# Two half steps per couple in the attention pipeline of a two-block kernel

## The chip, the core and the metric

The kernel runs on one core of a Trainium2 chip, as one launch. The metric is the device time of a run in microseconds (us). Five engines of the core work side by side, each through its own queue in order: TensorE (PE; its weight loads are listed apart, as PEld), VectorE (DVE), ScalarE (ACT), GpSimd (POOL) and SyncE (SP), which here issues nearly all the DMAs. They wait for each other through semaphores alone.

## What is computed

256 tokens of width 1024, in float32, go through two models of two layers each. The first block's layer has top-k sparse attention (8 heads), a short convolution, an RWKV-7 recurrence (8 heads) and a gated feed-forward part. The second block's layer, which most of the change concerns, is this:

```python
u = hdn @ w_in
qa, ka, va, za, qb, kb, vb, zb, ga, gb = split_cols(u)
ya = dilated_mixture(qa, ka, va)                  # 16 heads of 64
ya = ya * jax.nn.silu(za)
ob = diff_attention(qb[0::2], qb[1::2], kb[0::2], kb[1::2], vb, lam)   # 8 heads, two softmaxes each
yb = rms_norm_2(ob, subln_w, SUBLN_EPS) * (1.0 - lam_init) * jax.nn.silu(zb)
merged = jax.nn.sigmoid(ga) * (ya @ w_proj_a) + jax.nn.sigmoid(gb) * (yb @ w_proj_b)
return x + merged @ w_out
```

`yb @ w_proj_b` needs all heads of the second attention, `ya @ w_proj_a` all of the first, and everything else in `u` needs neither.

## The kernel before

Every weight product is done in three passes of a reduced float32: the weights are loaded by DMA into `raw` and split by ACT (L184, `whi`) and DVE (L185, `wlo`) into a high and a low part; PE multiplies the parts by those of the activations, in the token-major form (L244 to L246, 512 columns each) or the feature-major one (L206 to L208, 256 columns). A "weight product" below is one such matmul. There are two buffers of `raw`, three of `whi`, three of `wlo`, and three PSUM banks (`mm`) for the results.

An attention is cut into couples of softmaxes, each in three pieces. The scores piece (`softmax_pair`): PE writes scores (L445), DVE evicts them with the mask and the row's extreme (L451), ACT takes the exponential (L454), DVE the reciprocal of the sum (L457). The probabilities piece: DVE scales (L465; in the second attention also L1411 and L1414), PE transposes (L486), ACT copies the result (L488, `pt`). The products piece: PE multiplies by the values (L496 and L498 in the first block and in the dilated attention, L1421 to L1423 in the differential one), and ACT takes the result out (L1424) and sums its squares (L1427). One half of an attention in the second block, `half`, is four couples. After the four couples of a half of the differential attention come a reciprocal root (`rstd`, L275 with L261 to L271), eight products on DVE (L1437), eight transposes (L393) and the split of the result (L1359, L1360), which the second half of the rows of `w_proj_b` multiplies.

`pipelined` runs four couples so that in step i the scores of couple i, the products of couple i-2 and the probabilities of couple i-1 are issued. It is a generator. Each number it yields is a length in a planner's units: `interleave` keeps a clock for each stream of work, advances the stream that is earliest, and so writes the program's order. In the second block two streams run, `bulk` with the weight products, which yields 10.4 after a token-major group of 48 and 5.2 after a feature-major one, and `attend`, whose step is `2 * TUNE["a2"]` or `2 * TUNE["b2"]` (9.95 and 10.49). In the first block there are three, `rwkv`, `attend` with `2 * TUNE["a1"]` times 0.746, and `bulk`. Streams also stop for each other: in the second block `bulk` does not begin the projection by `w_proj_b` before `attend` has finished, and in the first it does not begin the attention's gate and branch products before that. Within this order a compile-time scheduler may still move an instruction ahead where its inputs are ready earlier.

In the first block's recurrence a solve on DVE ends in transposes (L933, L935), then PE, ACT and DVE hand each other small steps: L942, L947 (the inverse), and for each of four stretches of tokens L962 and L965, L972, L977, L990 and L993.

In the second block, 176.8 of the planner's units of `bulk` stand ahead of the projections in the first layer, and each projection has 20.8.

Of the kernel before, what the change touches and what calls it, by code (L numbers as in the profile page):

```python
# [116 lines left out]
class Core:  # L117
# [349 lines left out]
    def pipelined(self, heads, step):  # L467

        n = len(heads)
        state = {}  # L470
        for i in range(n + 2):
            if i < n:
                state[i] = heads[i][0]()
                yield step / 3
            if 0 <= i - 2 < n:
                heads[i - 2][2](state.pop(i - 2))
                yield step / 3
            if 0 <= i - 1 < n:
                state[i - 1] = heads[i - 1][1](state[i - 1])
                yield step / 3  # L480

    def flip_probs(self, p):

# [1020 lines left out]
```

## Time and profile before

| | |
|---|---|
| three runs | 1722.09, 1722.85 and 5703.48 us, median 1722.85 |
| the profiled execution | 1723.79 us, of which the span from the first to the last instruction is 1722.0 |
| mean granted TensorE clock | 0.985 |
| busy, share of the span | PE 98%, PEld 86%, DVE 72%, ACT 56%, POOL 2% |
| first block, both layers | about 0 to 1010 us |
| second block, two layers | about 1010 to 1350 and 1350 to 1722 us |

The table is read so: PE's busy time counts from the start of a matmul to its modelled end, and matmuls overlap, so the distance from start to start, and whether PE waits for anybody, tell more than the share.

### The profile page before, as it was taken

What the parts mean: (1) busy time and instruction counts of PE and PEld (TensorE: products, weight loads), DVE (VectorE), ACT (ScalarE), POOL (GpSimd) and SP (SyncE); (2) the same over time, 40 slices, a digit from 0 to 9 for tenths busy, and PEclk for the clock granted to TensorE, in tenths of its full rate; (3) what the DMA queues carried; (4) which work ended last, traced back from release to release, by engine and by line L of the source; (5) the groups of instructions that cost most, each with busy time, mean ns of one, the idle gap of its engine ahead of it and who ended that gap; (6) DMA issues with size and microseconds to landing.
All of it is one profiled execution on the core that took longest, in us unless ns stands there. A gap on an engine that the chain in (4) does not pass through costs nothing.

```text
span 1722.0 us, 28074 instructions
## 1 busy us (share of the span) xinstructions
PE 1683.5 (98%) x11080; PEld 1488.3 (86%) x11080; DVE 1240.7 (72%) x2482; ACT 957.9 (56%) x1692; POOL 26.0 (2%) x56
## 2 busy tenths in 40 slices
PE   8999999999999999999999999999999999999998
PEld 7988889899989988889899988787878887878786
DVE  6589946789957689847789857576666665666666
ACT  6554733556646544734555656666664556666643
POOL 3000000001000000000000000000000000000000
PEclk9999989999999999989999999999999999999999
DMA  7543413566556443324555565344545554444553
GB/s 227 166 125 101 132 52 122 180 191 193 174 189 194 147 134 111 112 62 147 171 190 178 179 210 175 133 148 152 168 155 171 187 171 139 155 151 150 168 171 135
DMA packets 196436, 267.73 MB, mean 155 GB/s; under 512 B 6618, under 2 KB 129820, under 8 KB 196304
## 3 DMA queue, kind: packets, MB, share of 16 engines
q1 hardware_dynamic: 193040, 262.81, 47.4%
q10 hardware_dynamic: 2368, 2.89, 0.5%
q8 instruction: 87, 1.43, 0.4%
q0 software_dynamic: 896, 0.24, 0.1%
q14 instruction: 45, 0.37, 0.1%
HBM read 264.87 MB, written 1.05 MB: 154 GB/s over the span
## 4 chain that ended last, share of the span: by engine, by line
PE 83%; DVE 9%; DMA 3%; ACT 3%; issue 2%; ACTq 0%; SPq 0%; DVEq 0%
PE ps L246 13%; PE ps L244 13%; PE ps L245 13%; PE ps L206 11%; PE ps L208 10%; PE ps L207 10%; DVE wlo L185 3%; PE ps L445 2%; PE ps L393 2%; DMA raw<-in_w_in_dram 1%; ACT whi L184 1%; PE ps L486 1%; PE ps L496 1%; PE ps L650 1%; DMA raw<-in_w_out_dram 1%
## 5 line engine op out<-in xcount | busy, mean ns | idle before, releaser
L185 DVE TENSOR_TENSOR wlo<-raw,whi 128x1024 fp32r<-128x1024 f32 (+2 forms) x504 | 606.4, 1207 | 311.1 <-ACT whi L184 297.3
L184 ACT ACTIVATE whi<-raw 128x1024 fp32r<-128x1024 f32 (+2 forms) x504 | 525.7, 1046 | 522.1 <-PE ps L246 205.4
L206 PE MATMUL ps<-op,whi 128*128 128x256 f32 x1824 | 523.5, 287 | 1.0 <-ACT whi L184 1.0
L208 PE MATMUL ps<-op,wlo 128*128 128x256 f32 x1824 | 519.6, 285 | 4.6 <-DVE wlo L185 4.5
L207 PE MATMUL ps<-op,whi 128*128 128x256 f32 x1824 | 519.9, 285 | 2.3 <-DVE op L199 2.3
L244 PE MATMUL ps<-whi,op 128*128 128x512 f32 (+2 forms) x1104 | 433.6, 393 | 0.8 <-ACT qtok L1203 0.8
L245 PE MATMUL ps<-wlo,op 128*128 128x512 f32 (+2 forms) x1104 | 427.1, 387 | 2.8 <-DVE wlo L185 2.8
L246 PE MATMUL ps<-whi,op 128*128 128x512 f32 (+2 forms) x1104 | 428.7, 388 | 0.0
L206 PEld LDWEIGHTS ps<-op,whi 128*128 128x128 f32 x1824 | 350.5, 192 | 8.4 <-issue 5.2
L208 PEld LDWEIGHTS ps<-op,wlo 128*128 128x128 f32 x1824 | 350.6, 192 | 7.7 <-DVE wlo L185 5.4
L207 PEld LDWEIGHTS ps<-op,whi 128*128 128x128 f32 x1824 | 350.6, 192 | 5.5 <-DVE op L199 3.1
L244 PEld LDWEIGHTS ps<-whi,op 128*128 128x128 f32 x1104 | 208.6, 189 | 42.5 <-issue 2.0
L245 PEld LDWEIGHTS ps<-wlo,op 128*128 128x128 f32 x1104 | 208.9, 189 | 41.8 <-DVE wlo L185 3.8
L246 PEld LDWEIGHTS ps<-whi,op 128*128 128x128 f32 x1104 | 208.4, 189 | 41.8 <-issue 1.7
L454 ACT ACTIVATE e<-e,m 128x128 f32<-128x128 f32 (+1 forms) x160 | 70.8, 445 | 14.0 <-DVE m L451 13.8
L451 DVE CUSTOM_DVE_ANT_0 e<-ps,consts 128x128 f32<-128x128 f32 (+1 forms) x128 | 38.7, 351 | 10.4 <-PE ps L445 8.1
L199 DVE TENSOR_TENSOR op<-xt,op 128x512 fp32r<-128x512 f32 x48 | 32.2, 687 | 18.8 <-ACT op L198 18.8
L715 DVE SCALAR_TENSOR_TENSOR glu<-ps,vec,glu 128x254 f32<-128x254 f32 x72 | 34.4, 478 | 1.4
L445 PE MATMUL ps<-qT 64*128 64x256 f32 (+1 forms) x256 | 35.0, 351 | 0.3
L714 DVE SCALAR_TENSOR_TENSOR glu<-ps,vec,glu 128x255 f32<-128x255 f32 x72 | 34.3, 477 | 0.2
L488 ACT COPY pt<-ps 128x384 f32<-128x384 f32 x64 | 28.8, 481 | 9.5 <-PE ps L486 5.5
L713 ACT ACTIVATE glu<-ps,vec 128x256 f32<-128x256 f32 x72 | 33.0, 458 | 1.5 <-DVE glu L715 1.5
(345 smaller groups left out, 1521.9 us busy)
## 6 DMA issues: line engine op xcount, KB each, us to landing
raw<-in_w_in_dram SPq DMA_DIRECT2D x130, 1024.0 KB, 5.2
raw<-in_ffn_up_dram SPq DMA_DIRECT2D x44, 1024.0 KB, 5.1
raw<-in_ffn_down_dram SPq DMA_DIRECT2D x20, 1024.0 KB, 5.1
raw<-in_w_out_dram SPq DMA_DIRECT2D x16, 1024.0 KB, 5.1
raw<-in_w_branch_dram SPq DMA_DIRECT2D x24, 512.0 KB, 3.5
raw<-in_w_proj_a_dram SPq DMA_DIRECT2D x8, 1024.0 KB, 5.1
raw<-in_w_proj_b_dram SPq DMA_DIRECT2D x8, 1024.0 KB, 5.0
raw<-in_w_in_dram SPq DMA_DIRECT2D x8, 768.0 KB, 4.6
```

Of the source, the lines that this page charges most:

```text
L184: nc.scalar.activation(out=hi, in_=v, func=AF.Copy)
L185: nc.vector.tensor_tensor(out=lo, in0=v, in1=hi.bitcast(F32), op=ALU.subtract)
L206: self.nc.tensor.matmul(ps, lhsT=hi[:, k], rhs=xh, start=k == 0, stop=False)
L207: self.nc.tensor.matmul(ps, lhsT=hi[:, k], rhs=xl, start=False, stop=False)
L208: self.nc.tensor.matmul(ps, lhsT=lo[:, k], rhs=xh, start=False, stop=k == nk - 1)
L244: self.nc.tensor.matmul(ps[t][:, :n], lhsT=xh, rhs=hi, start=kk == first, stop=False)
L245: self.nc.tensor.matmul(ps[t][:, :n], lhsT=xh, rhs=lo, start=False, stop=False)
L246: self.nc.tensor.matmul(ps[t][:, :n], lhsT=xl, rhs=hi, start=False, stop=kk == last)
L393: self.nc.tensor.transpose(ps[:, a, 128 * t:128 * t + 128], src[t][:, 128 * k:128 * k + 128], self.ident)
L445: nc.tensor.matmul(ps[b][:, a:a + n], lhsT=qt[r, 128 * t:128 * t + 128], rhs=kt[r, 0:n], start=True, stop=True)
L451: nc.vector.tensor_tensor_reduce(out=e[:, a:a + n], in0=ps[b][:, a:a + n], in1=mask[:, a:a + n], scale=1.0, scalar=3e38, op0=ALU.add, op1= ...
L454: nc.scalar.activation(out=e[:, a:a + n], in_=e[:, a:a + n], func=AF.Exp, scale=-1.0, bias=m[:, t:t + 1], accum_out=z[:, 2 * b + t:2 * b + ...
```

## The change

```diff
         for i in range(n + 2):
             if i < n:
                 state[i] = heads[i][0]()
-                yield step / 3
             if 0 <= i - 2 < n:
                 heads[i - 2][2](state.pop(i - 2))
-                yield step / 3
+            yield step / 2
             if 0 <= i - 1 < n:
                 state[i - 1] = heads[i - 1][1](state[i - 1])
-                yield step / 3
+            yield step / 2
```

Scores and the products of two couples back are now issued without a yield between them, and a yield is made whether or not its piece was there. All lines behind it are one lower in the changed kernel. The function has three callers: the first block's attention and both attentions of the second.

A row of the order names line, operation, output and inputs, and the size of the output. On PE, in the first half of the differential attention of the second block's first layer, where `ident` is the identity for a transpose and `e` holds the probabilities, there stood:

```order
L445 MATMUL ps<-qT 128x128 x2
L445 MATMUL ps<-qT 128x256 x2
L1421 MATMUL ps<-v,pt 128x128
L1422 MATMUL ps<-v,pt 128x128
L1423 MATMUL ps<-v,pt 128x128
L486 MATMUL ps<-ident,e 128x128 x3
```

and now:

```order
L485 MATMUL ps<-ident,e 128x128 x3
L445 MATMUL ps<-qT 128x128 x2
L445 MATMUL ps<-qT 128x256 x2
L1420 MATMUL ps<-v,pt 128x128
L1421 MATMUL ps<-v,pt 128x128
L1422 MATMUL ps<-v,pt 128x128
```

The six rows stand between two groups of 48 weight products in both; the transposes moved from behind to ahead.

On PE at the end of the last half of the same layer, where `o` is the attention's output, there stood 40 weight products between the last L1423 and the transposes of `o`, of which these are the last three:

```order
L244 MATMUL ps<-whi,op 128x512
L245 MATMUL ps<-wlo,op 128x512
L246 MATMUL ps<-whi,op 128x512
L393 MATMUL ps<-ident,o 128x128 x8
L244 MATMUL ps<-whi,op 128x512
```

and now:

```order
L1420 MATMUL ps<-v,pt 128x128
L1421 MATMUL ps<-v,pt 128x128
L1422 MATMUL ps<-v,pt 128x128
L245 MATMUL ps<-wlo,op 128x512
L246 MATMUL ps<-whi,op 128x512
L244 MATMUL ps<-whi,op 128x512
L245 MATMUL ps<-wlo,op 128x512
L246 MATMUL ps<-whi,op 128x512
L1420 MATMUL ps<-v,pt 128x128
L1421 MATMUL ps<-v,pt 128x128
L1422 MATMUL ps<-v,pt 128x128
L393 MATMUL ps<-ident,o 128x128 x7
```

No weight product stands there any more between the last couple and the transposes. From the first score of that half to the seventh transpose of `o` there are 30 weight products, in pieces of one to nine, where there were 192 up to the eighth; 24 are the half of the projection by `w_proj_b` for the first 512 columns that needs the earlier couples alone, and six belong to the next 512 columns. The second layer has the same rows.

On PE in the first block's first layer, where the recurrence's solve ends (`t`, `ti`, `xs`, `wsb` and `uv` are its tiles, `av` the attention's values), there stood:

```order
L942 MATMUL ps<-t_2180,gm 32x32 x32
L207 MATMUL ps<-op,whi 128x256
L208 MATMUL ps<-op,wlo 128x256
L206 MATMUL ps<-op,whi 128x256
L207 MATMUL ps<-op,whi 128x256
L208 MATMUL ps<-op,wlo 128x256
L947 MATMUL ps<-ti,xs 32x32 x32
L965 MATMUL ps<-uv,gm 64x64 x8
L206 MATMUL ps<-op,whi 128x256
L207 MATMUL ps<-op,whi 128x256
L208 MATMUL ps<-op,wlo 128x256
L486 MATMUL ps<-ident,e 128x128 x5
```

and now:

```order
L941 MATMUL ps<-t_2160,gm 32x32 x32
L495 MATMUL ps<-pt,av 64x256
L497 MATMUL ps<-pt,av 64x128 x2
L485 MATMUL ps<-ident,e 128x128 x3
L946 MATMUL ps<-ti,xs 32x32 x32
L964 MATMUL ps<-uv,gm 64x64 x8
L485 MATMUL ps<-ident,e 128x128 x5
L971 MATMUL ps<-wsb,ti 64x64 x8
L485 MATMUL ps<-ident,e 128x128 x4
L976 MATMUL ps<-uv,bkt 128x128 x4
L992 MATMUL ps<-uv,gm 64x64 x8
L961 MATMUL ps<-sd_94,ar 64x128 x4
```

Eight weight products left the gaps of this step, and attention products and transposes that stood earlier moved into them. In the second layer no weight product stood there before either.

## Rows read from the trace of the kernel before

**Rows 1.** The page's part 1: busy us, share of the span, instructions.

```profile
PE 1683.5 (98%) x11080; PEld 1488.3 (86%) x11080; DVE 1240.7 (72%) x2482; ACT 957.9 (56%) x1692; POOL 26.0 (2%) x56
```

**Rows 2.** Stages: from:to, length, busy us by engine (instructions), PEclk, DMA share, GB/s.

```profile
1240.00:1320.00 80.00, 79.93 (x393) 64.68 (x392) 51.39 (x125) 47.98 (x102) 0.00 (x0) 1.00 0.48 158
```

**Rows 3.** Timeline of PE: start, us, instruction; around the last half's first scores.

```profile
1257.76 0.39 PE L244 MATMUL ps<-whi,op 128*128 128x512 f32 x1
...
1261.62 0.39 PE L246 MATMUL ps<-whi,op 128*128 128x512 f32 x1
1261.94 0.93 PE L445 MATMUL ps<-qT 64*128 64x128 f32 x8
1262.79 0.50 PE L244 MATMUL ps<-whi,op 128*128 128x512 f32 x1
```

**Rows 4.** Timeline of DVE through the same half, with idle time before and its releaser.

```profile
1262.89 0.29 DVE L451 CUSTOM_DVE_ANT_0 e<-ps,consts 128x128 f32<-128x128 f32 x1 [1.25 <-PE ps L445]
...
1264.01 1.22 DVE L185 TENSOR_TENSOR wlo<-raw,whi 128x1024 fp32r<-128x1024 f32 x1
...
1279.51 0.18 DVE L457 RECIPROCAL z<-z 128x4 f32<-128x4 f32 x1
...
1280.32 0.74 DVE L1414 SCALAR_TENSOR_TENSOR e<-e,z 128x128 f32<-128x128 f32 x2
...
1306.96 0.17 DVE L275 TENSOR_SCALAR oss<-oss 128x8 f32<-128x8 f32 x1 [2.01 <-ACT sq L1427]
...
1310.21 2.19 DVE L1437 SCALAR_TENSOR_TENSOR o<-o,oss,zb 128x128 f32<-128x128 f32 x8
1312.32 2.35 DVE L185 TENSOR_TENSOR wlo<-raw,whi 128x1024 fp32r<-128x1024 f32 x2
```

**Rows 5.** Timeline of PE: the last couple's transposes and products, and the output's transposes.

```profile
1302.62 0.49 PE L486 MATMUL ps<-ident,e 128*128 128x128 f32 x3
...
1304.92 0.49 PE L1421 MATMUL ps<-v,pt 128*128 128x128 f32 x2
...
1305.47 0.39 PE L1423 MATMUL ps<-v,pt 128*128 128x128 f32 x2
...
1314.82 1.03 PE L393 MATMUL ps<-ident,o 128*128 128x128 f32 x8
```

**Rows 6.** Timeline of ACT: a copy of probabilities, and the output's first splits.

```profile
1304.11 0.49 ACT L488 COPY pt<-ps 128x384 f32<-128x384 f32 x1
...
1315.98 1.25 ACT L1359 ACTIVATE op<-ps,sw 128x512 fp32r<-128x512 f32 x2
```

**Rows 7.** Stages around PE's stalls in the first block, columns as in rows 2.

```profile
163.00:166.00 3.00, 0.45 (x3) 0.24 (x3) 2.97 (x7) 2.06 (x3) 0.15 (x1) 1.00 0.00 0
166.00:170.00 4.00, 4.00 (x22) 4.00 (x23) 4.00 (x14) 1.32 (x3) 0.00 (x0) 0.57 0.34 88
...
221.00:234.00 13.00, 12.63 (x122) 11.48 (x120) 3.44 (x5) 3.38 (x7) 0.00 (x0) 0.50 0.03 12
...
726.00:743.00 17.00, 15.36 (x165) 14.32 (x163) 2.54 (x5) 3.56 (x7) 0.00 (x0) 0.50 0.10 33
```

**Rows 8.** Timeline of PE: the recurrence's first step, in both layers of the first block.

```profile
216.18 3.79 PE L942 MATMUL ps<-t,gm 32*32 32x32 f32 x64 [0.80 <-DVE z L457]
...
234.54 1.04 PE L962 MATMUL ps<-sd,ar 128*64 128x128 f32 x8
...
724.14 3.79 PE L942 MATMUL ps<-t,gm 32*32 32x32 f32 x64 [2.08 <-DVE t L935]
...
741.98 1.55 PE L962 MATMUL ps<-sd,ar 128*64 128x128 f32 x8
```

**Rows 9.** PE's waits, 697 to 810 us: who for whom, us, times, longest.

```profile
PE ps L942 <- DVE t L935: 2.1, 1, 2.1
...
PE ps L972 <- DVE wsb L968: 0.9, 1, 0.9
PE ps L977 <- DVE uv L973: 0.8, 1, 0.8
```

## The prediction

> **What bounds the kernel now.** Read the page's busy times first: PE works 98% of the span, DVE 72%, ACT 56% [rows 1]. Then the stage in which the second block's first layer runs the last half of its differential attention: PE is busy 79.93 of 80 us at a granted clock of 1.00, while DVE and ACT have 29 and 32 us to spare [rows 2]. The attention's chain (scores, eviction, exponential, scaling, transposes, copy, products) is long and thin, but weight products lie beside all of it, so its waits cost nothing. In rows 3 the weight products start 0.227 us apart ((1261.62 - 1257.76) / 17), and eight score matmuls take 0.85 us between two of them. Where PE does lose time is the first block: one stall in which it works 0.45 of 3 us, followed by 4 us at a clock of 0.57, and one recurrence step in each layer with a clock of 0.50 [rows 7]. So the kernel is bound by PE's work, and a change that keeps that work can only cost or gain where PE waits or where the clock is low.
>
> **The change, part by part.** No matmul, split or load is added or removed.
>
> *Scores beside the values' products.* In the second block's steady part this takes nothing away: scores and products of two back stood in a row before too, and PE waits for nobody there. The transposes move ahead of the scores, with 48 weight products (48 x 0.227 = 10.9 us) on either side, several times the length of a head's chain on DVE and ACT. Price 0; without that cover it would be the wait priced next. The DMA issues of SP and POOL keep their order, so no load starts later by its queue.
>
> *The pace.* This is the part that I charge. Before, a yield of a third of a step followed each piece; four couples have twelve pieces, so a half advances the planner's clock by four steps. Now each of six iterations yields two halves: six steps. The steps being 9.95 and 10.49, two halves of each attention take 2 x 4 x (9.95 + 10.49) = 163.5 units before and 245.3 after. The other stream has 176.8 + 20.8 = 197.6 units before it must stop for the attention's end. Before, attention ended first, with weight products left to cover its tail; now the weight products run out during the last half. The built order says so: 30 weight products are left between the last half's first score and the transposes of `o`, against 192.
>
> So I walk that half, from its first score, by its slowest engine.
> (a) The first eviction starts 0.95 us after the first score [rows 3, 4].
> (b) DVE then works through four heads. From the first eviction to the end of its statistics 1.12 us pass (1264.01 - 1262.89), and from the reciprocal to the end of the scaling 1.55 (1280.32 + 0.74 - 1279.51): 2.67 a head, 10.7 for four. One weight split of 1.22 lies in between [rows 4], and about 1.3 is lost because the second head's scores are queued behind nine weight products (9 x 0.227 = 2.0). The last scaling ends at about 14.1.
> (c) Transposes 0.49 and copy 0.49 follow [rows 5, 6]; the last products stand behind five weight products (1.1) which wait for a split of some 1.2 on DVE. They start at about 16.5.
> (d) From these products to the reciprocal root 2.04 pass (1306.96 - 1304.92) [rows 4, 5]: 18.5.
> (e) Root and eight products take 5.36 to the next split (1312.32 - 1306.96); something else lay within it, of which I take off one split (2.35 / 2 = 1.17) [rows 4], since few remain: 4.2, so 22.7.
> (f) Last transposes and the first of the two splits of the output (1.25 / 2) [rows 5, 6], about 0.9: 23.6 us until dense products can resume.
>
> PE's own work in these 23.6 us: scores 4 x 0.85 = 3.4; transposes 4 x 0.49 = 2.0; products 4 x 0.8 = 3.2 (0.55 between the starts in rows 5 and one more matmul); output transposes 1.0; 30 weight products 6.8. Sum 16.4. PE stands idle for 7.2 us, in each of two layers: **+14.4 us**. The new waits are transposes for the scaling, products for the copy, output transposes for the eight products, and dense products for the output's split; behind each on PE's queue there is only the next small piece, so whoever waits there stops PE.
>
> *The clock behind it.* The stall in rows 7 was followed by 4 us at 0.57, a loss of up to 4 x 0.43 = 1.7 us. The longest gap here (from d to f, some 5 us with eight transposes in it) is of that kind: 1.7 a layer, **+3.4**. Its bounds are nothing, and half speed through the whole stretch: then the 16.4 us of work become 32.8 and the idle time disappears into them.
>
> The Trainium skill ("Perfetto Trace Analysis", "Optimization Strategy") says that where the most contended engine changes over time, interleaving the regimes may help. By it the tail, a DVE regime, should lie among weight products, as it did: PE at 79.93 of 80 us agrees, and the change takes that apart at the end of each layer.
>
> *Block 1.* The same function feeds the first block. Eight weight products leave the gaps of the first layer's recurrence step, and four attention products and twelve transposes move in. The step from L942 to L962 takes 18.4 us in the first layer, with weight products in it, and 17.8 in the second, without (234.54 - 216.18, 741.98 - 724.14) [rows 8]; so the eight hid in the step, and taken out they cost 8 x 0.227 / 2 = 0.9 at some other place (256 columns, half of those in rows 3). The rest of the chain waits little: 2.1 us once, then under 1 [rows 9]. Against it, the moved transposes now fill gaps where they used to cost. I take **+1**. Bounds: +8, if the moved weight products also uncover other waits (the 3.8 us in rows 9 a second time, and 1.7 of clock, with the 0.9 and as much again for products that move in later steps); and -8, about half of what the two steps lose by the clock (below).
>
> **Sum:** 14.4 + 3.4 + 1 = 18.8 us on the profiled execution's 1723.79: 1742.6. The median of the runs is 0.94 lower, so I forecast 1742.
>
> **Rivals.**
>
> *The clock falls early in the tail* (slower). If the first wait of the tail already drops the clock to half and the small matmuls never bring it back, PE's work is the bound: 32.8 us instead of 16.4, +16.4 a layer, +32.8 for two, 1757 on the profile with Block 1 at nothing, 1764 with Block 1 at its +8. For it: in both recurrence steps PE is busy 12.63 of 13 and 15.36 of 17 us with small matmuls and still has 0.50 [rows 7], so that a chain of small steps can stay at half speed. Against: scores are large and weight products stand between the first couples. It decides from the point at which the clock has fallen before the third couple's scores. The Trainium skill ("TensorE: Matmul & The Clock Gate", "What's actually happening") says that the default state is throttled and activity releases it; by that this rival needs only that the thin activity is not enough, and rows 7 agree.
>
> *Block 1's gain pays for it* (not slower). The two recurrence steps spend 13 and 17 us at 0.50 [rows 7]. If attention work in their gaps brought the clock to 1.00, up to 6.5 + 8.5 = 15 us would return, with 3.8 of waits [rows 9]: 18.8 - 1 - 18.8, that is 1723. For it: more matmuls in the gaps. Against: they are small ones, of the kind that ran at half clock there before.
>
> *The change doesn't do what it says for the time.* If the scores and products stood together before and the tail stays covered because DVE's and ACT's spare time shortens it, nothing changes: 1723, perhaps 1727 with the clock. For: the steady part's order, and 29 and 32 us of spare time in rows 2. Against: 30 weight products are 6.8 us, and the walk needs 23.6.
>
> *Batches gain.* The Trainium skill ("Perfetto Trace Analysis", "Matmul Optimizations") wants matmuls back to back, since the engine scales with utilization; by that, small matmuls put together would run faster. Rows 2 leave nothing to gain: clock 1.00, 0.07 us idle in 80. It would give 1720, with Block 1 as now.
>
> **How the numbers follow.** About 2% (1688 to 1757) is what a measurement of this kernel can tell from no change. Forecast (1731 to 1756) 0.75; clock early 0.13; Block 1 pays 0.05; tail covered 0.06; batches 0.01. The forecast's low end: the walk without the 1.3 in (b) and the 1.2 in (c) leaves 4.7 idle, 9.4 for two layers, no clock loss and Block 1 at -2. The range of 8 in 10 leaves out the cheap cases, nearly all of the early clock, and reaches a little below the forecast's own low end: 1729 to 1757. Within 2%: the 0.75, the cheap cases' 0.12 less the 0.01 below, and what is left of the early clock, 0.87. Slower by over 2%: nearly all of the early clock, which also has Block 1's cost, 0.12. Faster by over 2% needs more than all half-clock stretches return: 0.01.
>
> **What would show it.** In the changed profile, each layer of the second block should have one stretch of some 24 us, from the last half's first scores to the first dense products behind the transposes of `o`, in which PE idles 5 to 8 us, waiting for the scaling (now L1413), the copy (L487), the eight products (L1436) and the output's split (L1358), with a granted clock below 1.00 at its end. The rest of the second block should stay at PE 99% and clock 1.00. The first block should end within some us of where it did. The forecast is wrong if the stretch holds at 1.00 without idle time, if its clock is 0.50 throughout, or if the first block's end moves by over 8 us.

## The result and the profile after

The changed kernel took 1739.47 us (median of four runs, 1738.11 to 1741.21), against 1722.78 of the kernel before (median of four); the ratio is 1.0097, with a 95% interval of 1.0084 to 1.011. The ratio leaves out the one run of the kernel before that took 5703 us. The profiled execution has a span of 1737.1 us, 15.1 more than before. The page's part 1 of the changed kernel, which answers to [rows 1]:

```profile
PE 1689.7 (97%) x11080; PEld 1491.1 (86%) x11080; DVE 1240.1 (71%) x2482; ACT 957.5 (55%) x1692; POOL 26.0 (1%) x56
```

The counts of PE, DVE, ACT and POOL are the same, and DVE's, ACT's and POOL's work too. So the 15 us are waiting, or the same work taking longer. To place them, take two marks that both kernels have, transposes of `h` on PE: one set at the end of the first block, and one at the end of the second block's first layer (a layer's end has two such sets, one for each 512 columns; these are the second and the first of theirs, so the stretch between the marks is nearly a layer, but not quite one). Timeline of PE before:

```profile
1030.96 0.44 PE L393 MATMUL ps<-ident,h 128*128 128x128 f32 x2
...
1361.61 0.44 PE L393 MATMUL ps<-ident,h 128*128 128x128 f32 x2
```

and after:

```profile
1030.62 0.44 PE L393 MATMUL ps<-ident,h 128*128 128x128 f32 x2
...
1369.32 0.44 PE L393 MATMUL ps<-ident,h 128*128 128x128 f32 x2
```

The first block ends 0.3 us earlier; between the marks pass 338.70 us instead of 330.65, +8.05; what is left to the end of the span is 367.8 instead of 360.4, +7.4. The loss stands in the two layers of the second block, in nearly equal parts. Between the marks the two kernels look so, before and after (columns as in [rows 2]):

```profile
1030.96:1361.61 330.65, 329.74 (x1717) 267.02 (x1717) 217.94 (x508) 196.25 (x385) 0.00 (x0) 1.00 0.49 160
1030.62:1369.32 338.70, 333.04 (x1717) 268.53 (x1716) 217.97 (x508) 196.29 (x385) 0.00 (x0) 0.99 0.48 156
```

PE's idle time grows from 0.91 to 5.66 us, by 4.75, and its busy time by 3.30 for the same matmuls. Within this stretch, the stages of the changed kernel (columns as in [rows 2]):

```profile
1240.00:1300.00 60.00, 60.00 (x293) 48.65 (x292) 34.36 (x81) 35.64 (x77) 0.00 (x0) 1.00 0.51 164
1314.50:1340.20 25.70, 21.01 (x108) 14.54 (x108) 19.52 (x81) 16.42 (x61) 0.00 (x0) 0.97 0.25 82
1338.70:1342.10 3.40, 3.38 (x11) 2.51 (x11) 2.26 (x5) 1.37 (x2) 0.00 (x0) 0.50 0.02 5
1340.20:1350.20 10.00, 10.00 (x42) 8.04 (x41) 6.07 (x9) 3.87 (x4) 0.00 (x0) 0.91 0.28 91
```

From 1240 to 1300 us PE never pauses. From the last half's first score to the dense products, 25.7 us, it is busy 21.0, idle 4.7. The clock falls to 0.50 at the end of this stretch and stays there for 3.4 us; so the 10 us behind it, in which PE is busy throughout, have a mean of 0.91. PE's timeline through the stretch, which answers to [rows 3, 5]:

```profile
1314.52 0.93 PE L445 MATMUL ps<-qT 64*128 64x128 f32 x8
1315.38 0.50 PE L244 MATMUL ps<-whi,op 128*128 128x512 f32 x1
...
1317.32 0.39 PE L246 MATMUL ps<-whi,op 128*128 128x512 f32 x1
1317.78 1.48 PE L445 MATMUL ps<-qT 64*128 64x128 f32 x8
...
1319.61 0.92 PE L445 MATMUL ps<-qT 64*128 64x128 f32 x4
...
1330.12 0.30 PE L485 MATMUL ps<-ident,e 128*128 128x128 f32 x1 [0.77 <-DVE e L1413]
...
1333.00 0.49 PE L1420 MATMUL ps<-v,pt 128*128 128x128 f32 x2
...
1333.55 0.39 PE L1422 MATMUL ps<-v,pt 128*128 128x128 f32 x2
1337.77 2.02 PE L393 MATMUL ps<-ident,o 128*128 128x128 f32 x7 [3.84 <-DVE o L1436]
1339.58 0.80 PE L244 MATMUL ps<-whi,op 128*128 128x512 f32 x1
1340.17 0.41 PE L393 MATMUL ps<-ident,o 128*128 128x128 f32 x1
1340.24 0.78 PE L245 MATMUL ps<-wlo,op 128*128 128x512 f32 x1
```

A number in brackets is idle time and who ended it. There is one long gap, 3.84 us, between the last couple's products and the transposes of `o`, and behind it matmuls of 512 columns take 0.8 us instead of 0.39. The scores of the third and the fourth couple come in rows of four records, each of which takes as long (0.92 us) as the first couple's eight (0.93). DVE, timeline of the same stretch, which answers to [rows 4]:

```profile
1315.28 1.23 DVE L185 TENSOR_TENSOR wlo<-raw,whi 128x1024 fp32r<-128x1024 f32 x1 [0.30 <-ACT whi L184]
1316.42 0.74 DVE L1359 SCALAR_TENSOR_TENSOR op<-ps,sw,op 128x512 fp32r<-128x512 f32 x1
1317.09 0.28 DVE L451 CUSTOM_DVE_ANT_0 e<-ps,consts 128x128 f32<-128x128 f32 x1
...
1329.63 0.74 DVE L1413 SCALAR_TENSOR_TENSOR e<-e,z 128x128 f32<-128x128 f32 x2
...
1335.05 0.17 DVE L275 TENSOR_SCALAR oss<-oss 128x8 f32<-128x8 f32 x1 [3.53 <-ACT sq L1426]
...
1337.27 2.19 DVE L1436 SCALAR_TENSOR_TENSOR o<-o,oss,zb 128x128 f32<-128x128 f32 x8
```

The root waits for the last products and ACT's squares, and PE waits for root and products: the chain that used to be covered. PE's waits in the whole changed kernel (who for whom, us, times, longest):

```profile
PE ps L393 <- DVE o L1436: 7.7, 2, 3.8
PE ps L941 <- DVE t L934: 4.7, 2, 2.4
...
PE ps L485 <- DVE e L1413: 1.5, 2, 0.8
```

The first and the third of these were not among PE's waits before. The copy of the probabilities (L487) and the output's split (L1358), which the prediction also named, do not appear among PE's waits. The second belongs to the first block's recurrence step, whose timeline on PE answers to [rows 8]:

```profile
214.15 3.79 PE L941 MATMUL ps<-t,gm 32*32 32x32 f32 x64 [2.40 <-DVE t L934]
...
233.10 1.04 PE L961 MATMUL ps<-sd,ar 128*64 128x128 f32 x8
...
723.57 3.80 PE L941 MATMUL ps<-t,gm 32*32 32x32 f32 x64 [2.26 <-DVE t L934]
...
742.28 1.06 PE L961 MATMUL ps<-sd,ar 128*64 128x128 f32 x8
```

and whose stages answer to [rows 7]:

```profile
219.00:232.00 13.00, 13.00 (x121) 11.35 (x121) 1.81 (x4) 4.94 (x15) 0.00 (x0) 0.50 0.03 9
725.00:743.00 18.00, 18.00 (x187) 15.89 (x186) 4.26 (x7) 7.23 (x19) 0.00 (x0) 0.55 0.09 30
```

The step takes 18.95 and 18.71 us where it took 18.36 and 17.84, and the clock in it is still about half. PE has no pause in it any more, but what fills the pauses is attention work at that clock.

### The profile page after: what moved, and what is told of

It reads as the page before. It is cut to its first block, busy times and chain, and to the rows that moved or that the text cites. A ratio compares the mean times of both kernels' runs of the same rounds, so it can differ in the third digit from the quotient of the medians.

```text
span 1737.1 us, 28067 instructions
## 1 busy us (share of the span) xinstructions
PE 1689.7 (97%) x11080; PEld 1491.1 (86%) x11080; DVE 1240.1 (71%) x2482; ACT 957.5 (55%) x1692; POOL 26.0 (1%) x56
## 3 DMA queue, kind: packets, MB, share of 16 engines
q8 instruction: 87, 1.43, 0.3%
## 4 chain that ended last, share of the span: by engine, by line
PE 80%; DVE 9%; DMA 5%; ACT 4%; issue 1%; ACTq 0%; SPq 0%; DVEq 0%
PE ps L244 13%; PE ps L246 13%; PE ps L245 13%; PE ps L206 10%; PE ps L208 10%; PE ps L207 10%; DVE wlo L185 3%; DMA raw<-in_w_in_dram 3%; PE ps L445 2%; ACT whi L184 2%; PE ps L393 2%; PE ps L485 1%; DMA raw<-in_w_out_dram 1%; DMA raw<-in_w_branch_dram 1%; PE ps L495 1%
## 5 line engine op out<-in xcount | busy, mean ns | idle before, releaser
L485 PE MATMUL ps<-ident,e 128*128 128x128 f32 x192 | 33.1, 294 | 1.5 <-DVE e L1413 1.5
```

Of the source, the lines that this page charges most:

```text
L485: self.nc.tensor.transpose(ps[:, 128 * j:128 * j + 128], p[:, 128 * j:128 * j + 128], self.ident)
```

## Experiments

The kernel before was run again beside the experiments. Its median was 1723.75 us beside the first four (new order at the old pace, old order at the new pace, one block at a time), 1723.07 beside the next four (the pace in between, without the chain, the first filler) and 1723.61 beside the last four; each ratio below is to the runs of its own group. A diff shows the line that matters, not the whole edit.

**The new order at the old pace.** In the changed `pipelined`, both yields:

```diff
-            yield step / 2
+            yield step / 3
```

> New order of the pieces, but each of the two yields is a third of a step, so that four couples take four steps as in the kernel before. Theory (the pace costs, the order does not): the tail of the last half is covered again by some 44 weight products behind the last couple, and the time is that of before, 1723 us (1720 to 1726). Rival (scores beside the values' products cost by themselves): it stays near the 1739 us of the changed kernel.

Measured: 1725.79 us, ratio 1.0018 (1.0009 to 1.0027). With the pace undone, the loss is gone but for 2 us by the medians and 3 by the ratio; the rival's 1739 is refuted. That is more than I expected of the order. In its trace 332.2 us pass between the marks, 1.5 more than before, and 361.1 behind them, 0.7 more, and PE has two waits that the kernel before did not have (PE's waits of this kernel):

```profile
PE ps L495 <- ACT pt L487: 0.9, 4, 0.2
...
PE ps L1420 <- ACT sq L1426: 0.7, 4, 0.2
```

The values' products directly behind the scores come a little before the copy, or the emptied bank, that they need. These waits are 1.6 of the 2.2 us.

**The old order at the new pace.** In the kernel before, all three yields:

```diff
-                yield step / 3
+                yield step / 2
```

> Old order with three yields, each half a step instead of a third: the pace of the changed kernel without its order. Theory (pace): weight products run out in the last half of both layers of the second block, 1738 us (1733 to 1744). Rival (order): 1723 us.

Measured: 1739.4 us, ratio 1.0092 (1.0077 to 1.0107). The pace alone gives the whole loss, without any change of order among scores and products. Between the marks its trace has 338.86 us (1367.85 - 1028.99), as in the changed kernel.

**One block at a time.** A second method with the old body of `pipelined` serves either the two callers of the second block, or that of the first (one of the three calls is shown):

```diff
-            yield from k.pipelined([head(i) for i in range(4)], 2 * TUNE["b2"])
+            yield from k.pipelined3([head(i) for i in range(4)], 2 * TUNE["b2"])
```

> The change in the first block's attention alone; the second block keeps three yields. Theory: the first block ends within 1 us of where it did, 1722.5 us (1720 to 1726), since what leaves the gaps of the recurrence step is made good by what moves in. Rival (the first block gains some us at its half-clock steps and hides part of the tail's cost): 1715 to 1719 us.

> The change in both attentions of the second block alone. Theory: the whole cost is here, 8 us in each layer, 1739 us (1736 to 1742). Rival (the first block carries a part of the cost or hides one): at least 3 us from the changed kernel's 1739.5.

Measured: 1724.57 us, ratio 1.0003 (0.9994 to 1.0013), with the change in the first block alone; 1738.99 us, ratio 1.0088 (1.0071 to 1.0105), with the change in the second alone. The second block carries the cost; the first block's share lies between -1 and +2 us and can't be told from nothing.

**The pace in between.** The changed `pipelined` with other fractions of a step; first four couples in five steps, then in four and a half (both yields; one is shown):

```diff
-            yield step / 2
+            yield step * 5 / 12
```

> The changed order with yields of 5/12 of a step, so that four couples take five steps: two halves of each attention are 204.4 of the planner's units against 197.6 of the weight stream. The built order has 16 weight products between the last couple and the eighth transpose of the output, 3.6 us, where the chain from the last products to the transposes took 4.8 in the changed kernel. Theory (cover by weight products): 1 to 3 us a layer stay, 1726 to 1731 us. Rival (any excess over the stream's length uncovers the whole tail): 1737 us or more.

> The changed order with yields of 3/8 of a step: four and a half steps for four couples, 184 of the planner's units against 197.6. The built order has 41 weight products behind the last couple, as many as before. Theory: fully covered, like the version with four steps, 1723 to 1727 us, and no gap in PE ahead of the output's transposes. Rival (each half step more costs its share of the 16 us): 1728 us or more.

Measured: 1726.75 us, ratio 1.002 (1.0008 to 1.0031), for five; 1720.5 us, ratio 0.9983 (0.9974 to 0.9992), for four and a half (`step * 0.375`). With five steps a part of the gap is left (timeline of PE in the kernel with five steps):

```profile
1325.48 0.39 PE L1422 MATMUL ps<-v,pt 128*128 128x128 f32 x2
...
1330.72 0.30 PE L393 MATMUL ps<-ident,o 128*128 128x128 f32 x1 [1.43 <-DVE o L1436]
```

It is 1.43 us, since most of the time between these two rows is filled by 15 weight products. The second layer has the same gap, but not the same clock (timeline of PE in the second layer, and the stage behind the gap in the first):

```profile
1673.86 0.30 PE L393 MATMUL ps<-ident,o 128*128 128x128 f32 x1 [1.40 <-DVE o L1436]
```

```profile
1332.20:1335.50 3.30, 3.30 (x10) 2.49 (x10) 2.76 (x4) 0.96 (x2) 0.00 (x0) 0.50 0.52 197
```

In the first layer the clock falls to 0.50 behind the gap, in the second it stays at 1.00 (from 1674 to 1677 us), and nothing here shows why. The first loses 2.0 us against the kernel before (332.67 between the marks), the second 0.4 (360.79 behind them), so that the fall's price in this kernel is some 1.6 us, an estimate from the two. The loss, then, is no steady price per half step: between four and a half and five steps, where the attention's length in the planner's units passes that of the weight stream, the gap appears, and at six steps it has grown to 3.84 us. Where between these points it sets in was not measured. That four and a half steps are faster than the kernel before I had not expected.

**Without the chain at the end.** In the last half, root and eight products are left out, so that the kernel computes something else:

```diff
-            r = k.rstd(ss, 128, 1e-5)
+            r = None if half else k.rstd(ss, 128, 1e-5)
...
-            for i in range(4):
+            for i in range(0 if half else 4):
```

> The changed kernel without the reciprocal root and its eight products in the last half of each layer (that half of the second attention's output stays unnormalised and ungated). Theory (the uncovered chain on DVE is the cost): the transposes of the output follow the copy instead of the eight products, 3 to 3.5 us earlier, and with the shorter gap the clock stays up, another 1 to 1.7: 4 to 5 us a layer, 1729 to 1732 us. Rival (PE's end there is set by something else, as loads or splits of weights): 1737 us or more.

Measured: 1727.21 us, ratio 1.0029 (1.0018 to 1.004). 12.3 us come back, more than the 8 to 10 that I expected; the time lies below the range. The transposes of the first three couples' output now run ahead of the last couple's products, as the timeline of PE in this kernel shows.

```profile
1330.08 1.06 PE L393 MATMUL ps<-ident,o 128*128 128x128 f32 x6
1331.91 0.38 PE L1420 MATMUL ps<-v,pt 128*128 128x128 f32 x2
...
1333.28 0.38 PE L393 MATMUL ps<-ident,o 128*128 128x128 f32 x2
```

Loads and splits of weights are as many here as in the changed kernel, and the last transposes follow the last products after 1.4 us instead of 4.8. What follows there does not wait for weights.

**What the clock costs.** A first attempt fills the gap with matmuls that depend on the last couple's probabilities alone (`last[0]` is its `pt`; the lines that set it are left out):

```diff
             yield from k.pipelined([head(i) for i in range(4)], 2 * TUNE["b2"])
+            if half:
+                ps = k.bank(k.rk, 512)
+                for _ in range(28):
+                    nc.tensor.matmul(ps[:, 0:128], lhsT=last[0][:, 0:128], rhs=v[:, 0, 0:128], start=True, stop=True)
```

> The changed kernel with 28 extra matmuls per layer (the last couple's first product again, into a free PSUM bank that nobody reads) between the last products of the last half and the transposes of its output, where PE stands idle for 3.8 us. They add about 3 us of PE work inside that gap and no result. Theory (the gap lets the clock fall to half for 3.4 us behind it, as in the changed kernel's trace): the clock stays at 1.00 and 1.2 to 1.7 us a layer come back, 1736 to 1737 us. Rival (what follows the gap waits for ACT's splits of the output, not for the clock): 1739 to 1740 us.

Measured: 1740.05 us, ratio 1.0105 (1.009 to 1.012), as the rival says, but it decides nothing. The fillers (L1437; the couple's own products begin with L1423 here) did not stay in the gap (timeline of PE in this kernel):

```profile
1331.24 1.28 PE L1437 MATMUL ps<-v,pt 128*128 128x128 f32 x10
1332.54 0.49 PE L1423 MATMUL ps<-v,pt 128*128 128x128 f32 x2
...
1333.31 5.30 PE L1437 MATMUL ps<-v,pt 128*128 128x128 f32 x46
1338.45 1.04 PE L393 MATMUL ps<-ident,o 128*128 128x128 f32 x8
```

Ten of them took the place of weight products ahead of the last couple, and the rest ran for 5.1 us (1338.45 - 1333.31), longer than the gap. So a second attempt reads the output's last copy, which places the fillers by data:

```diff
-                for _ in range(28):
-                    nc.tensor.matmul(ps[:, 0:128], lhsT=last[0][:, 0:128], rhs=v[:, 0, 0:128], start=True, stop=True)
+                for _ in range(13):
+                    nc.tensor.matmul(ps[:, 0:128], lhsT=o[:, 1, 384:512], rhs=v[:, 0, 0:128], start=True, stop=True)
```

> The changed kernel with 13 extra matmuls a layer that read the output's last copy, so that they can only run between that copy and the eight products' end (2.8 us at 0.109 us for each of their 26 records); every other instruction keeps its place, which the earlier filler did not allow (ten of its records ran before the last couple's products and six weight products behind it). Their result is not used. Theory (half a clock for 3.4 us behind the gap is a part of the cost): the clock stays at 1.00 and 1.0 to 1.7 us a layer come back, 1736 to 1737.5 us. Rival (what follows the gap waits for ACT's split of the output anyway): 1739 to 1740 us.

Measured: 1737.99 us, ratio 1.0076 (1.0061 to 1.0091), half a microsecond above the theory's range. The timeline of PE and the stage behind it, in this kernel:

```profile
1334.50 0.49 PE L1420 MATMUL ps<-v,pt 128*128 128x128 f32 x2
...
1335.89 3.17 PE L1434 MATMUL ps<-v,o 128*128 128x128 f32 x26 [0.46 <-ACT o L1423]
1339.28 1.81 PE L393 MATMUL ps<-ident,o 128*128 128x128 f32 x7 [0.21 <-DVE o L1440]
...
1369.65 0.44 PE L393 MATMUL ps<-ident,h 128*128 128x128 f32 x2
```

```profile
1341.50:1351.00 9.50, 9.50 (x44) 7.63 (x43) 6.71 (x9) 3.88 (x4) 0.00 (x0) 1.00 0.29 107
```

The clock is 1.00 where it was 0.91. From the last products to the second mark pass 35.15 us (1369.65 - 1334.50) against 36.32 in the changed kernel (1369.32 - 1333.00): the clock cost 1.2 us in the first layer. In the second it cost 0.5, from the last products to the end of the span (1736.9 - 1682.30 against 1737.1 - 1681.97). The span is nearly that of the changed kernel all the same, because the first block, in which nothing differs, ended 1.7 us later in this execution (1032.29). The medians, 1737.99 against 1739.47, point the same way, but the intervals of the ratios overlap, so the size rests on the traces. The seven transposes of `o` take 1.81 us at full clock too, against 1.03 for eight in [rows 5]: they come as the eight products come.

**Where the gain at four and a half steps lies.** The old order with that pace (all three yields; one is shown), and the new order with it in one block alone (the other block as before; not shown):

```diff
-                yield step / 3
+                yield step * 0.375
```

> The old order of the pieces, with yields of 3/8 of a step: twelve of them are four and a half steps. The new order at this pace ran at 1720.5 us, faster than the kernel before. If the pace made that gain, this kernel has it too: 1719 to 1722 us. If the order made it, this one is at 1723 to 1726 us, since it has 22 weight products behind the last couple where the other had 42.

> The new order at four and a half steps in the second block alone; the first block's attention as in the kernel before. If the gain of the version with four and a half steps lies in the second block: 1720 to 1721.5 us. If it lies in the first (whose trace ended 1.7 us earlier): 1722 to 1724 us.

> The new order at four and a half steps in the first block's attention alone, the second block as before: 1720 to 1721.5 us if the gain lies here, 1722 to 1724 us if it lies in the second block.

Measured: the old order 1718.57 us, ratio 0.9965 (0.9953 to 0.9978); the new order in the second block alone 1721.96 us, ratio 0.9986 (0.9977 to 0.9996); in the first alone 1720.87 us, ratio 0.9983 (0.9974 to 0.9992). The first is a little below its range, which speaks for the pace; the second lies between its two ranges, the third in the one for the first block. By their ratios each block would give 2 to 3 us with the new order, though together (0.9983) they give no more than one. The trace of the kernel with the second block alone does not bear that out: its two layers are 0.1 and 0.5 us shorter than before (330.58 between the marks, 359.91 behind them), and its first block, the same as before, ended 1.75 us earlier (1029.21). The first block of the changed kernel ended anywhere between 1029.16 and 1032.29 us in five executions with the same instructions, so a gain of 2 or 3 us in the first block can't be told from that by a trace.

The old order at four and a half steps is the fastest of all, 0.35% below the kernel before. Its timeline of PE at the two marks:

```profile
1028.12 0.44 PE L393 MATMUL ps<-ident,h 128*128 128x128 f32 x2
...
1357.75 0.44 PE L393 MATMUL ps<-ident,h 128*128 128x128 f32 x2
```

Between them pass 329.63 us instead of 330.65, and behind them 359.35 instead of 360.39. The two traces in which the second block is as before repeat the 330.65 within 0.3 us, so about 2 us of the gain are shown to lie in the second block; what makes them was not followed up. The first block ends 2.8 us earlier than before, no more than its executions differ by.

## Why the prediction was right

The forecast was 1742 us, the result 1739.5, by the step that was charged: **the pace**. That a measurement could tell no less than about 2% from no change was too careful: the interval of 1.0084 to 1.011 leaves no doubt of the loss.

*What bounds the kernel.* Right: PE stays the bound before the tail, busy 60.00 of 60 us at a clock of 1.00, and the loss is where it waits.

*Scores beside the values' products, price 0.* Right for this kernel, since the old order at the same pace ran at 1739.4. Not quite right as a rule: at four steps the order cost 2 to 3 us, 1.6 of them in short waits of the products for ACT, and at four and a half the old order is 1.9 us faster by the medians.

*The walk through the last half.* The stretch took 25.7 us instead of 23.6, and the step that was off is (a): before DVE could take the first eviction it had a weight split (1.23) and the split of the half before (0.74) in its queue, so it began 2.57 us after the first score (1317.09 - 1314.52), not 0.95. That cost PE little, since nine weight products lay beside it. From there on the walk of DVE held. (b) From the first eviction to the end of the last scaling: 13.3 us (1329.63 + 0.74 - 1317.09), walked as 13.15. (c) From there to the last products 2.6, walked as 2.4. (d) From these to the root 2.05, walked as 2.04. (e) Root and eight products 4.4 (1337.27 + 2.19 - 1335.05), walked as 4.2. (f) 0.8, walked as 0.9.

*Idle time, +14.4.* The size held, but not all of it is idle time. The layers lost 8.05 and 7.4 us; less 1.2 and 0.5 for the clock, 6.9 are left in each, where 7.2 were forecast. Yet PE idles only 4.7 of the 25.7 us, a little under the 5 to 8 named as a sign, and its idle time grew by 4.75 between the marks and by 4.63 behind them. A part of the rest is waiting that the profile counts as work: the transposes of `o` come one by one as DVE's products come, and take 1.81 and 0.27 us at full clock (in the kernel with the second filler) against 1.03 in [rows 5], 1.1 more. With 4.75 of idle time and 1.2 of the clock that makes 7.0 of the 8.05; the last 1.0 is spread over smaller differences and was not followed up. The walk put PE's own work at 16.4 us, and the profile counts 21.0. Half of the difference is its term of 4 x 0.85 for the scores: from the start of their rows to the next matmul they take 0.86, 1.40, 1.70 and 1.70 us in the four couples, 5.7 in sum, since in the third and the fourth four records take as long as eight did. They took 4.0 in the same half before.

*The waits.* Two of the four that were named appeared: transposes for the scaling (1.5 us) and output transposes for the eight products (7.7). Products did not wait for the copy, nor dense products for the output's split.

*The clock behind it, +3.4.* Right in its kind, too large: I took the 4 us at 0.57 of [rows 7] as lost in full, 1.7 a layer. The fall covered 3.4 us here as well, but part of that ran while the transposes waited for DVE's products anyway. The second filler showed 1.2 us in the first layer and 0.5 in the second.

*Block 1, +1.* The trace gives -0.3, the run with the change there alone +0.8 (ratio 0.9994 to 1.0013). Nothing that can be measured, and the recurrence step grew by 0.6 and 0.9 us without the block growing. Two details of the working were off without consequence: the order shows three attention products that move in, not four, and of the twelve transposes six stood in the first layer's step before; and the terms of the bound of +8 add up to 7.3.

*The sum.* 18.8 forecast on the profiled execution, 15.1 found: 1.7 of the difference from the clock (3.4 - 1.7), 1.3 from Block 1 and 0.7 from the term of idle time (14.4 - 13.7).

*The rivals.* The clock fell late, behind the gap, and not in the first third of the tail, so the time stayed below 1757. The first block's steps stayed at 0.50 and 0.55, so nothing came back there. The tail was not covered by DVE's spare time, and the half of the change that puts batches together gained nothing. Of the sentences of the Trainium skill in the prediction, that on interleaving regimes ("Perfetto Trace Analysis", "Optimization Strategy") is the one that the runs bear out: the same chain of DVE and ACT cost nothing beside 40 weight products, 1.43 us of idle time beside 15, and 3.84 beside none.

## What to carry to other kernels

A yield in a planner's stream is a price: turning three yields of a third, made only where a piece was issued, into two halves that are always made lengthened the attention by half, and that, not the new order, made nearly all of the loss. Add up such lengths for each stream and compare the sums: as long as the thin stream ends first, its chains cost next to nothing; past that point the last chain stands bare, once a layer. And where a tail is bare, walk it by its slowest engine with durations from the covered case; here it held within a few tenths a step, except at its head, where the queues still held older work. The work of the engine that is the bound is less safe to carry over: its scores took 5.7 us in the tail instead of 3.4.

## What the runs showed of the hardware

After a gap of 3.84 us, in which PE did nothing, the granted clock fell to 0.50 while the transposes behind it ran, and stayed there for 3.4 us; with 26 small matmul records in that gap it stayed at 1.00, though PE still paused for 0.46 and 0.21 us. A gap of 1.43 us was followed by 0.50 as well, in one layer, while one of 1.40 us in the next layer was not. Matmuls that compute nothing useful can hold the clock, but here they bring back 1.2 us of an 8 us loss in one layer and 0.5 of 7.4 in the other: the waiting itself was the larger part.
